# Where the matmul operands of a two-layer encoder start in SBUF, modulo 256 bytes

## The chip, the core and the metric

The kernel runs on one core of one Trainium2 chip. The metric is the device time of one execution in microseconds (us), lower is better. Engines are called PE (TensorE; its weight loads are a row of their own, PEld), DVE (VectorE), ACT (ScalarE), POOL (GpSimd) and SP (which here issues DMAs).

## The reference

A hybrid encoder trunk of two layers on two request groups of 256 tokens (512 tokens together, model width 1024), all in float32:

```python
def encoder_layer(x, c, cos, sin, p):
    ...
    h = rmsnorm(x, p['ln1_g']) * (1 + sc1) + sh1
    (q_down, kv_down, rg_x, rg_gate, gdn_qkv, gdn_z,
     gdn_alpha, gdn_beta, gates) = split_cols(h @ p['w_in'], IN_SPLITS)
    ...
    for n, o_n in enumerate((o_mla, o_rg, o_gdn)):
        term = gates[:, :, n] * (o_n @ p['w_branch'][n])
        mixed = term if mixed is None else mixed + term
    x = x + gt1 * (mixed @ p['w_out'])
    h2 = rmsnorm(x, p['ln2_g']) * (1 + sc2) + sh2
    up = dwconv_centred(h2 @ p['ffn_w_up'], p['ffn_conv_w'], p['ffn_conv_b'])
    u_lin, u_gate = jnp.split(up, 2, axis=-1)
    x = x + gt2 * ((jax.nn.silu(u_gate) * u_lin) @ p['ffn_w_down'])
    return x
```

The three branches are latent attention (MLA), a gated linear recurrence (RG-LRU) and a gated delta rule (GDN). Most of the arithmetic is products of a weight matrix with 512 columns of activations.

## The kernel before, in words

Activations lie transposed: 128 channels on the partitions, the 512 tokens along the row. Every weight matrix is cut into units of 128x128; all units of a layer stand in one list in the order in which they are used, eight units to a chunk. A chunk (128 x 1024 float32, 512 KB) is loaded by SP into one of three `raw` buffers (`prefetch`, L369), then split into two float32r parts (`split_chunk`, L375): ACT rounds it into `wh`, DVE subtracts and writes the rest into `wl`. Each of the two has two buffers that are used in turn. The split of a chunk is called when the unit that stands six units ahead of it is handed out (`AHEAD`). Activations are split in the same way: `hh`/`hl` (the normalised input), `ch`/`cl` and `oh`/`ol` (attention), `xch`/`xcl` and `goh`/`gol` (the other branches), `mh`/`ml` (the mixed branches) and `ah`/`al` (FFN).

`mm3` (L400) makes each unit's product out of three matmuls in one pass each: high weights with high activations, high weights with low activations, low weights with high activations. The weights are the stationary operand (loaded by LDWEIGHTS, 128 columns of 4 bytes), the activations are the moving operand (512 columns of 4 bytes; `gemm` takes 256 columns where a job works on one request group, `g` 0 or 1). Only the values of the attention (`values`, L780) turn this round: there the split weights move.

`SIZE` gives the units of a job, `JOBS` the order of jobs; `BRANCHES` has how often each job comes:

```python
SIZE = {"in6": 48, "gq": 8, "gk": 8, "gv": 8, "uq": 3, "uk": 2, "pad": 2, "uv": 8,
        "gate": 8, "br": 4, "x": 8, "g": 8, "b": 2, "z": 8, "out3": 24, "out": 8, "up3": 24, "up": 8,
        "down": NFF, "close": 0, "mid": 0, "close2": 0}
```

PE's instructions stand in a list written out by hand. Between the jobs' matmuls a small driver puts in the steps of the branches (attention, delta rule, norms, the modulation `mod`), each when a modelled clock has passed the waiting time that a table (`SLACK`) gives it. These steps run in float32 matmuls.

SBUF buffers come from pools that lie one behind the other in each partition; a buffer starts at a multiple of 32 bytes. The constants (`cs`, `pv` and others) end at byte 27,168, which is 32 modulo 256; the pools `xm`, `h` and `w` follow, and their buffers are multiples of 2,048 bytes. So `hh`, `hl`, `raw`, `wh` and `wl` all start at 32 modulo 256. The pool `small` behind them shifts what comes next. In the built program the split buffers that PE reads start at these places modulo 256:

| operand | role | before | after |
|---|---|---|---|
| `hh` `hl` `ch` `cl` `oh` `ol` `xch` `xcl` `goh` `gol` | moving | 32 | 0 |
| `mh` `ml` `ah` `al` | moving | 224 | 0 |
| `wh` first, second buffer | weights | 32, 32 | 128, 32 |
| `wl` first, second buffer | weights | 32, 32 | 192, 224 |

A unit's weights start at a multiple of 512 bytes within their buffer, and a request group's activations at 0 or 1,024, so the places of the table hold for each of them. The GDN's `kq`, both operands of `gdn_gram`, starts at 96 before and at 0 after.

Of the kernel before, what the change touches and what calls it, by code (L numbers as in the profile page):

```python
# [8 lines left out]
F32 = mybir.dt.float32  # L9
F32R = mybir.dt.float32r  # L10
# [8 lines left out]
P = 128  # L19
# [215 lines left out]
def _body(es, tc, nc, xT, cT, wall, wmod, pvec, fng, cst, rope, xinit, yT, dbg):  # L235
# [3 lines left out]
    depth = pvec.shape[1]  # L239

    cp = es.enter_context(tc.tile_pool(name="const", bufs=1))
    xp = es.enter_context(tc.tile_pool(name="xm", bufs=8))
    hp = es.enter_context(tc.tile_pool(name="h", bufs=1))
    wp = es.enter_context(tc.tile_pool(name="w", bufs=2))
    sp = es.enter_context(tc.tile_pool(name="small", bufs=1))
    mm = es.enter_context(tc.tile_pool(name="mm", bufs=3, space=PSUM))
    aux = es.enter_context(tc.tile_pool(name="aux", bufs=5, space=PSUM))
    dp = es.enter_context(tc.tile_pool(name="dr", bufs=2, space=DRAM))


    cs = cp.tile([P, NCC], F32, name="cs")
# [26 lines left out]
    def debug(name, ap):  # L278
        if dbg is None or name not in dbg:
            return  # L280
        o = nc.dram_tensor("dbg_" + name, tuple(ap.shape), F32, kind="ExternalOutput").ap()
        nc.sync.dma_start(o, ap)
# [78 lines left out]


    NRAW = 3
    state = {"l": 0, "u": 0, "piece": None, "job": ""}

    loads, pieces = {}, {}


    def prefetch(at):  # L369
        if at not in loads:  # L370
            loads[at] = wp.tile([P, UC * P], F32, name="raw", tag="raw", bufs=NRAW)
            nc.sync.dma_start(loads[at], wall[at])
        return loads[at]

    def split_chunk(at):  # L375
        if at not in pieces:
            raw = prefetch(at)
            loads.pop(at)
            wh = wp.tile([P, UC * P], F32R, name="wh", tag="wh", bufs=2)
            wl = wp.tile([P, UC * P], F32R, name="wl", tag="wl", bufs=2)  # L380
            A.copy(wh, raw)  # L381
            sub(wl, raw, f32(wh))
            pieces[at] = (wh, wl)
# [287 lines left out]
    for l in range(depth):  # L671
# [62 lines left out]
        def low_rank():  # L734
            yield SLACK["low_rank"]
            ps = aux_tile((P, 8), "ssq")
            for e in range(2):
                token_sums(ps[:, 4 * e:4 * e + 4], lr["sq"][e])
            x = mp.tile([P, 8], F32, name="lrx", tag="lrx")
            r = lr["r"] = mp.tile([P, 8], F32, name="lrr", tag="lrr")  # L740
            for e, n in enumerate((3, 2)):
                V.tensor_scalar(x[:, 4 * e:4 * e + 4], ps[:, 4 * e:4 * e + 4], 0.5 / (n * P), 0.5 * EPS, ALU.mult, ALU.add)
            rsqrt(r, x)
            yield SLACK["lr_diag"]
            rs = aux_tile(name="spread")
            spread(rs, r[:, 4:8])
            for i in range(2):
                t = lr["raws"][i]
                stt(t, t, pcol("kv_norm_g", i), rs, ALU.mult, ALU.mult)
                ch = mp.tile([P, T], F32R, name="ch", tag="c2", bufs=10)  # L750
                cl = mp.tile([P, T], F32R, name="cl", tag="c2", bufs=10)
                split(t, ch, cl, pool=True)
                ckv.append((ch, cl))
            ev_ckv.set(SLACK["low_rank_out"])
# [259 lines left out]
        for job in JOBS:  # L1014
# [40 lines left out]
            elif k == "close":  # L1055
                for t in range(8):
                    debug(f"K{t}_{l}", Kt[:, t, :])
                    debug(f"Q{t}_{l}", Qt[:, t, :])
                mstack.close()
                RT, RS = 8, 2  # L1060
                ap = stack.enter_context(tc.tile_pool(name="rg", bufs=1))
# [19 lines left out]
                gdn.gated(hd, zt, oh, ol)  # L1081
            elif k == "mid":
                drv.until(gdn.ev_o)
                g2stack.close()
                ostack = ExitStack()
                op_ = ostack.enter_context(tc.tile_pool(name="outp", bufs=1, side="right"))
# [14 lines left out]
            elif k == "out3":  # L1101
                for d, ps in enumerate(gemms(ms_, 3)):
                    out_row(ps, d, 2)
            elif k == "out":
                d, g = ix
                out_row(gemm(ms_, g), d, g)
                if (d, g) == (7, 0):
                    h2 = {}
                    drv.spawn(early(l, 1, x1, sq, range(E2), h2, op_))
                elif (d, g) == (7, 1):  # L1110
                    wait(SLACK["norm"])
                    for us in sq.scale(1):
                        wait(us)
                    for k in range(8):
                        for g in ((1,) if k < E2 else (0, 1)):
                            modulated(l, 1, x1[k], sq.r[g], k, g, h2, op_, 4)
                    wait(SLACK["normed"])
                    drv.drain_spare()
                    ostack.close()
                    rstack.close()  # L1120
                    fstack = ExitStack()
                    fp = fstack.enter_context(tc.tile_pool(name="ffn", bufs=1))
            elif k == "up3":
                for n, ps in enumerate(gemms(hs(h2), 3)):
                    up(ps, n)
                if not last:
                    drv.spawn(mod_gen(l + 1, ((0, 1),), SLACK["mod2"]))
            elif k == "up":
                up(gemm(hs(h2)), ix[0])
            elif k == "down":  # L1130
                d, g = ix
                if d == 0:
                    sq = Norm(fp, 3)
                    if not last:
                        setup(l + 1)
                        xdram = dp.tile([P, 8, T], F32, name="xdram", tag="xdram")

                        def hraw(i):
                            half = []
                            for e in range(2):  # L1140
                                tag = "h%s%d" % ("hl"[e], i % 8)
                                t = hp.tile([P, T], F32, name="hraw", tag=tag)
                                nc.sync.dma_start(t, wmod[l + 1, i][:, e * T:(e + 1) * T])
                                half.append(t)
                            return tuple(half)
                        preload(l + 1, (2, 3), hraw)
                ps = gemm(acts, g)
                t = x1[d]
                for e in ((0, 1) if g == 2 else (g,)):
                    c = GS[e]  # L1150
                    stt(t[:, c], ps[:, c], modA[:, 3, d, e:e + 1], t[:, c], ALU.mult, ALU.add)
                    if not last:
                        nc.scalar.dma_start(xdram[:, d, c], t[:, c])
                sq.put(t, d, g)
                if g:
                    debug(f"x2_{d}_{l}", t)
                if last and d < 7:
                    A.activation(t, t, AF.Copy, scale=fg[:, d:d + 1])
                if (d, g) == (7, 0):
                    h = {}  # L1160
                    drv.spawn(result(x1, sq, 0) if last else early(l + 1, 0, x1, sq, (), h, fp))
# [16 lines left out]
class GDN:  # L1178
# [15 lines left out]

    def gates(self, ab):
        V, A, G, PE = self.V, self.A, self.G, self.PE
        g1, C = self.g1, self.C
        yield SLACK["ab"]
        ps = self.aux_tile((P, 4, 80), "gates")
        for t in range(4):  # L1200
            PE.transpose(ps[:, t, :], ab[0:80, t * P:(t + 1) * P], self.ident[0:80, 0:80])
        al = g1.tile([P, 4, 8], F32, name="al_", tag="al_")
        self.g = g1.tile([P, 4, 8], F32, name="g_", tag="g_")
        self.beta = g1.tile([P, 4, 8], F32, name="beta", tag="beta")
        dtb = self.pcol("dt_bias").unsqueeze(1).to_broadcast([P, 4, 8])
        nea = self.pr["nea"].unsqueeze(1).to_broadcast([P, 4, 8])
        V.tensor_tensor(al, ps[:, :, 64:72], dtb, ALU.add)
# [8 lines left out]
        for k, (m, d) in enumerate((("incf", 0), ("incb", 1), ("strf", 0), ("strb", 1))):  # L1216
            PE.matmul(pc[:, k, :], C(m), self.g[:, :, 4 * d:4 * d + 4], start=True, stop=True)

        self.negegc = g1.tile([P, 4, 4], F32, name="negegc", tag="negegc")
        self.ktail = g1.tile([P, 4, 4], F32, name="ktail", tag="ktail")  # L1220
        self.b1 = g1.tile([P, 4, 4], F32, name="b1", tag="b1")
        self.b2 = g1.tile([P, 4, 4], F32, name="b2", tag="b2")
        ex = g1.tile([P, 4, 16], F32, name="ex", tag="ex")
        A.activation(ex, pc, AF.Exp)
        exv = ex.rearrange("p k (g j h) -> p k g j h", g=2, j=2)
        bv = self.beta.rearrange("p (g j) e -> p g j e", j=2)
# [10 lines left out]

    def part(self, what, h, ps):
        V, A, G, PE = self.V, self.A, self.G, self.PE
        g1 = self.g1  # L1240
        if what == "q":
            self.heads[h] = dict(kq=g1.tile([P, 2, T], F32, name="kq", tag="kq", bufs=2),
                                 vt=g1.tile([P, 4, P], F32, name="vt", tag="vt", bufs=2),
                                 kd=g1.tile([P, 4, P], F32, name="kd", tag="kd", bufs=2),
                                 nrm=g1.tile([P, 3, 4], F32, name="nrm", tag="nrm", bufs=2),
                                 bR=g1.tile([P, 4, 2], F32, name="bR", tag="bR", bufs=2),
                                 ev_d=self.drv.event())
        hd = self.heads[h]
        c = g1.tile([P, T], F32, name="gc", tag="gc", bufs=2)
# [422 lines left out]
```

## Time and profile before

| | us |
|---|---|
| median of 3 runs (2043.85 to 2046.93) | 2044.58 |
| the profiled execution | 2049.36 |
| its span, first to last instruction | 2047.6 |
| PE busy in the span | 1988.4 |

The profile page gives busy time by engine and the chain of work that ended last; the trace answers with instructions in order of time, or grouped. A matmul's own time in the trace (0.39 us) is longer than the distance to the next one, because matmuls are pipelined: a stream's rate is read from the distance of starts.

### The profile page before, as it was taken

The numbers are of one execution on the slowest core, as the hardware profiler recorded it, in microseconds if no ns is written. First come the engines' busy times: TensorE is split into PE (matmuls) and PEld (weight loads), VectorE is DVE, ScalarE is ACT, GpSimd is POOL, SyncE is SP. The second block draws the span as 40 slices with busy tenths as digits, with TensorE's granted clock in tenths as the row PEclk, the third lists the DMA queues.
The fourth block names the chain that finished last, engine by engine and source line by source line (L and its number), as shares of the span: only waits on it lengthen the run. The fifth ranks groups of instructions, "written<-read, shape, count | busy, mean of one in ns | idle before, by whom it ended". The sixth has DMA issues, their size and how long they took to land.

```text
span 2047.6 us, 28679 instructions
## 1 busy us (share of the span) xinstructions
PE 1988.4 (97%) x11179; PEld 1560.5 (76%) x11179; DVE 1249.2 (61%) x2354; ACT 808.1 (39%) x1259; POOL 253.9 (12%) x519
## 2 busy tenths in 40 slices
PE   9999989999999999999999999799999999999998
PEld 4777756767787778888878777577678878888887
DVE  4675767744466766662357757785544677666434
ACT  3454355422333434442244534553323344444322
POOL 1100252222200100000011003523130010000000
PEclk9999999999999999999999999899999999999999
DMA  8232433334335343344333224333432533333333
GB/s 298 83 93 62 112 91 100 108 109 118 87 118 191 110 137 103 94 142 149 110 114 105 60 73 114 94 113 83 128 110 83 205 105 102 93 96 100 93 95 111
DMA packets 114135, 229.94 MB, mean 112 GB/s; under 512 B 52304, under 2 KB 57552, under 8 KB 114000
## 3 DMA queue, kind: packets, MB, share of 16 engines
q1 hardware_dynamic: 107376, 219.98, 35.9%
q10 hardware_dynamic: 6624, 8.14, 1.2%
q8 instruction: 88, 1.44, 0.3%
q14 instruction: 47, 0.39, 0.1%
HBM read 221.00 MB, written 7.08 MB: 111 GB/s over the span
## 4 chain that ended last, share of the span: by engine, by line
PE 84%; DVE 5%; POOL 4%; DMA 2%; issue 2%; ACT 2%; SPq 0%; POOLq 0%; DVEq 0%; ACTq 0%
PE mm_up L220 24%; PE mm_down L220 12%; PE mm_gate L220 11%; PE mm_br L220 6%; PE mm_out L220 4%; PE mm_in L220 3%; PE mod L220 3%; PE mm_z L220 2%; PE mm_gk L220 2%; PE mm_gv L220 2%; POOL xt L286 2%; POOL X L292 2%; PE mm_gq L220 2%; PE att_s L220 1%; PE gdn_rec L220 1%
## 5 line engine op out<-in xcount | busy, mean ns | idle before, releaser
L292 DVE TENSOR_TENSOR wl<-raw,wh 128x1024 fp32r<-128x1024 f32 x304 | 374.8, 1233 | 312.5 <-ACT wh L381 302.5
L381 ACT CAST wh<-raw 128x1024 fp32r<-128x1024 f32 x304 | 318.6, 1048 | 539.7 <-PE mm_down L220 131.9
L220 PE MATMUL mm_up<-hh,wh 128*128 128x512 f32 x704 | 277.0, 393 | 3.4 <-POOL hh L302 3.4
L220 PE MATMUL mm_up<-hl,wh 128*128 128x512 f32 x704 | 275.6, 391 | 0.0
L220 PE MATMUL mm_up<-hh,wl 128*128 128x512 f32 x704 | 275.4, 391 | 0.0
L295 DVE SCALAR_TENSOR_TENSOR cv<-mm_up,pv,cv 128x510 f32<-128x510 f32 x176 | 131.2, 748 | 68.4 <-ACT cv L544 65.3
L220 PEld LDWEIGHTS mm_up<-hh,wh 128*128 128x128 f32 x704 | 133.1, 189 | 38.1 <-issue 5.9
L220 PE MATMUL mm_gate<-hh,wh 128*128 128x512 f32 x384 | 160.7, 418 | 0.0
L220 PEld LDWEIGHTS mm_up<-hl,wh 128*128 128x128 f32 x704 | 133.0, 189 | 27.6 <-DVE hl L292 0.3
L220 PEld LDWEIGHTS mm_up<-hh,wl 128*128 128x128 f32 x704 | 132.9, 189 | 27.4
L220 PE MATMUL mm_gate<-hh,wl 128*128 128x512 f32 x384 | 150.3, 391 | 0.0
L220 PE MATMUL mm_gate<-hl,wh 128*128 128x512 f32 x384 | 150.3, 391 | 0.0
L220 PE MATMUL mm_down<-ah,wl 128*128 128x512 f32 (+1 forms) x396 | 146.1, 369 | 0.7 <-DVE wl L292 0.7
L220 PE MATMUL mm_down<-ah,wh 128*128 128x512 f32 (+1 forms) x396 | 146.1, 369 | 0.0
L220 PE MATMUL mm_down<-al,wh 128*128 128x512 f32 (+1 forms) x396 | 146.0, 369 | 0.0
L302 POOL TENSOR_SCALAR hh<-hn 128x256 fp32r<-128x256 f32 x64 | 34.0, 545 | 695.2 <-ACT hn L561 691.1
L544 ACT ACTIVATE cv<-mm_up,pv 128x512 f32<-128x512 f32 x88 | 68.4, 779 | 93.4 <-PE mm_up L220 93.4
L220 PEld LDWEIGHTS mm_gate<-hh,wh 128*128 128x128 f32 x384 | 72.3, 188 | 25.5 <-issue 12.5
L220 PEld LDWEIGHTS mm_down<-ah,wl 128*128 128x128 f32 x396 | 74.2, 187 | 15.1 <-DVE wl L292 0.9
L220 PEld LDWEIGHTS mm_down<-al,wh 128*128 128x128 f32 x396 | 74.3, 188 | 14.3
L220 PEld LDWEIGHTS mm_down<-ah,wh 128*128 128x128 f32 x396 | 74.2, 187 | 14.2
L220 PEld LDWEIGHTS mm_gate<-hh,wl 128*128 128x128 f32 x384 | 72.1, 188 | 16.1 <-DVE wl L292 0.2
(389 smaller groups left out, 3873.9 us busy)
## 6 DMA issues: line engine op xcount, KB each, us to landing
raw<-in_wall_dram SPq DMA_DIRECT2D x304, 512.0 KB, 3.6
raw<-in_wmod_dram SPq DMA_DIRECT2D x56, 512.0 KB, 3.7
mraw<-in_wmod_dram SPq DMA_DIRECT2D x16, 512.0 KB, 10.7
oraw<-in_wmod_dram SPq DMA_DIRECT2D x16, 512.0 KB, 7.5
hraw<-in_wmod_dram SPq DMA_DIRECT2D x16, 256.0 KB, 5.5
x<-in_xT_dram SPq DMA_DIRECT2D x8, 256.0 KB, 5.9
xr<-in_xT_dram ACTq DMA_DIRECT2D x8, 256.0 KB, 3.4
xdram<-x ACTq DMA_DIRECT2D x16, 128.0 KB, 2.3
```

What stands on the lines that cost most here:

```text
L220: return self.pe.matmul(out, lhsT, rhs, **kw)
L286: (eng or V).tensor_tensor(out, a, b, ALU.mult)
L292: (eng or V).tensor_tensor(out, a, b, ALU.subtract)
L295: V.scalar_tensor_tensor(out, a, s, b, op0, op1)
L302: G.tensor_scalar(hi, x, 1.0, 0.0, ALU.mult, ALU.add)
L381: A.copy(wh, raw)
L544: A.activation(dst, ps, AF.Identity, bias=bias, scale=w[lo])
```

## The change

No instruction is added, removed or moved: on all five engines the built program has the same instructions with the same waits in the same order; only SBUF addresses differ. The pool `small` moves ahead of `xm` and takes up the small buffers of the branches; unused fill buffers bring every pool to a multiple of 256 bytes. The two buffers of `wh` and of `wl` get names of their own, with fills between them, so that the four stand at four places.

```diff
     cp = es.enter_context(tc.tile_pool(name="const", bufs=1))
+    sp = es.enter_context(tc.tile_pool(name="small", bufs=1))
     xp = es.enter_context(tc.tile_pool(name="xm", bufs=8))
     hp = es.enter_context(tc.tile_pool(name="h", bufs=1))
     wp = es.enter_context(tc.tile_pool(name="w", bufs=2))
-    sp = es.enter_context(tc.tile_pool(name="small", bufs=1))
...
+    def fill(pool, size):
+        return pool.tile([P, size // 4], F32, name="fill", tag="fill", bufs=1)
+    fill(sp, 160)
+
+    fills = iter(range(8))
+
+    def shift(size):
+        wp.tile([P, size // 4], F32, name="fill", tag=f"fill{next(fills)}", bufs=1)
...
             loads[at] = wp.tile([P, UC * P], F32, name="raw", tag="raw", bufs=NRAW)
+            if not placed:
+                placed.append(True)
+                shift(128)
             nc.sync.dma_start(loads[at], wall[at])
...
-            wh = wp.tile([P, UC * P], F32R, name="wh", tag="wh", bufs=2)
-            wl = wp.tile([P, UC * P], F32R, name="wl", tag="wl", bufs=2)
+            b = state["buf"] = 1 - state["buf"]
+            wh = wp.tile([P, UC * P], F32R, name="wh", tag=f"wh{b}", bufs=1)
+            if not state["placed"][b]:
+                shift((64, 192)[b])
+            wl = wp.tile([P, UC * P], F32R, name="wl", tag=f"wl{b}", bufs=1)
+            if not state["placed"][b]:
+                shift((96, 32)[b])
+                state["placed"][b] = True
             A.copy(wh, raw)
             sub(wl, raw, f32(wh))
...
-            x = mp.tile([P, 8], F32, name="lrx", tag="lrx")
-            r = lr["r"] = mp.tile([P, 8], F32, name="lrr", tag="lrr")
+            x = sp.tile([P, 8], F32, name="lrx", tag="lrx")
+            r = lr["r"] = sp.tile([P, 8], F32, name="lrr", tag="lrr")
...
+                fill(mp, 96)
                 mstack.close()
...
+                fill(gdn.g2, 160)
                 g2stack.close()
...
+                    fill(op_, 224)
                     ostack.close()
```

The other lines of the diff move the GDN's small buffers (`al_`, `g_`, `beta`, `negegc`, `ktail`, `b1`, `b2`, `ex`, `nrm`, `bR`) from the pool `g1` to `small` in the same way.

## Rows read from the trace of the kernel before

**Rows 1.** Page, span and busy time by engine (us, share, instructions).

```profile
span 2047.6 us, 28679 instructions
PE 1988.4 (97%) x11179; PEld 1560.5 (76%) x11179; DVE 1249.2 (61%) x2354; ACT 808.1 (39%) x1259; POOL 253.9 (12%) x519
```

**Rows 2.** Page, the chain that ended last, by engine and by line.

```profile
PE 84%; DVE 5%; POOL 4%; DMA 2%; issue 2%; ACT 2%; SPq 0%; POOLq 0%; DVEq 0%; ACTq 0%
PE mm_up L220 24%; PE mm_down L220 12%; PE mm_gate L220 11%; PE mm_br L220 6%; PE mm_out L220 4%; PE mm_in L220 3%; PE mod L220 3%; PE mm_z L220 2%; PE mm_gk L220 2%; PE mm_gv L220 2%; POOL xt L286 2%; POOL X L292 2%; PE mm_gq L220 2%; PE att_s L220 1%; PE gdn_rec L220 1%
```

**Rows 3.** Busy us by stretch: PE, PEld, DVE, ACT, POOL, clock, DMA share, GB/s.

```profile
190.00:580.00 390.00, 371.56 (x2647) 284.12 (x2645) 235.14 (x461) 149.33 (x239) 103.41 (x216) 0.97 0.36 102
...
672.00:912.00 240.00, 240.00 (x1054) 191.52 (x1053) 159.37 (x205) 104.98 (x134) 3.20 (x5) 1.00 0.37 110
```

**Rows 4.** PE in order of time, FFN up: start us, length us, instruction.

```profile
821.30 0.39 PE L220 MATMUL mm_up<-hh,wh 128*128 128x512 f32 x1
821.52 0.39 PE L220 MATMUL mm_up<-hl,wh 128*128 128x512 f32 x1
821.75 0.39 PE L220 MATMUL mm_up<-hh,wl 128*128 128x512 f32 x1
...
823.34 0.39 PE L220 MATMUL mm_up<-hh,wh 128*128 128x512 f32 x1
```

**Rows 5.** PE in order of time, FFN down.

```profile
948.29 0.40 PE L220 MATMUL mm_down<-al,wh 128*128 128x512 f32 x1
948.52 0.40 PE L220 MATMUL mm_down<-ah,wl 128*128 128x512 f32 x1
948.76 0.39 PE L220 MATMUL mm_down<-ah,wh 128*128 128x512 f32 x1
...
950.39 0.39 PE L220 MATMUL mm_down<-al,wh 128*128 128x512 f32 x1
```

**Rows 6.** The chain in order of time: start us, us, pieces merged.

```profile
195.87 21.76 PE mm_br L220 x96
```

**Rows 7.** PE in order of time, warm-up (bfloat16), 16 matmuls merged.

```profile
7.75 3.62 PE L358 MATMUL warm<-zb 128*128 128x512 bf16 x16
```

**Rows 8.** PE in order of time, float32 products of the GDN, merged.

```profile
266.69 0.81 PE L220 MATMUL gdn_gram<-kq 128*128 128x256 f32 x3
```

**Rows 9.** PE's weight loads in order of time, where mm_up gives way to mod.

```profile
746.72 0.19 PEld L220 LDWEIGHTS mm_up<-hl,wh 128*128 128x128 f32 x1
746.95 0.19 PEld L220 LDWEIGHTS mm_up<-hh,wl 128*128 128x128 f32 x1
747.49 0.14 PEld L220 LDWEIGHTS mod<-raw,csil 128*32 128x32 f32 x4 [0.35 <-issue]
```

**Rows 10.** The tile mm_up in 747.36 to 747.47 us: length ns min/median/max.

```profile
L220 PE MATMUL mm_up<-hh,wl x1: 389/389/389, 747.2 to 747.2; 128*128 128x512 f32 x1
```

**Rows 11.** PE in order of time, five matmuls after a step of the GDN.

```profile
441.11 0.40 PE L220 MATMUL mm_gk<-hl,wh 128*128 128x512 f32 x1
441.34 0.39 PE L220 MATMUL mm_gk<-hh,wl 128*128 128x512 f32 x1
441.57 0.40 PE L220 MATMUL mm_gk<-hh,wh 128*128 128x512 f32 x1
441.80 0.39 PE L220 MATMUL mm_gk<-hl,wh 128*128 128x512 f32 x1
442.03 0.39 PE L220 MATMUL mm_gk<-hh,wl 128*128 128x512 f32 x1
```

**Rows 12.** Page, costliest groups: the split, and two of PE's (busy, mean ns).

```profile
L292 DVE TENSOR_TENSOR wl<-raw,wh 128x1024 fp32r<-128x1024 f32 x304 | 374.8, 1233 | 312.5 <-ACT wh L381 302.5
L381 ACT CAST wh<-raw 128x1024 fp32r<-128x1024 f32 x304 | 318.6, 1048 | 539.7 <-PE mm_down L220 131.9
L220 PE MATMUL mm_up<-hl,wh 128*128 128x512 f32 x704 | 275.6, 391 | 0.0
```

**Rows 13.** Page, DMA issues: the weight chunks (KB each, us to landing).

```profile
raw<-in_wall_dram SPq DMA_DIRECT2D x304, 512.0 KB, 3.6
```

**Rows 14.** What PE itself waited for: us, times, longest us.

```profile
PE gdn_l L220 <- DVE W L289: 12.6, 2, 6.4
PE gdn_rec L220 <- DVE Y L1466: 10.9, 2, 5.4
```

More of the change, by code (lines that the diff above doesn't have):

```diff
@@ L363, in _body @@
     NRAW = 3
-    state = {"l": 0, "u": 0, "piece": None, "job": ""}
-    loads, pieces = {}, {}
+    state = {"l": 0, "u": 0, "piece": None, "job": "", "buf": 1, "placed": [False, False]}
+    loads, pieces, placed = {}, {}, []
     def prefetch(at):
@@ L1196, in gates @@
         V, A, G, PE = self.V, self.A, self.G, self.PE
-        g1, C = self.g1, self.C
+        sp, C = self.sp, self.C
         yield SLACK["ab"]
@@ L1201, in gates @@
             PE.transpose(ps[:, t, :], ab[0:80, t * P:(t + 1) * P], self.ident[0:80, 0:80])
-        al = g1.tile([P, 4, 8], F32, name="al_", tag="al_")
-        self.g = g1.tile([P, 4, 8], F32, name="g_", tag="g_")
-        self.beta = g1.tile([P, 4, 8], F32, name="beta", tag="beta")
+        al = sp.tile([P, 4, 8], F32, name="al_", tag="al_")
+        self.g = sp.tile([P, 4, 8], F32, name="g_", tag="g_")
+        self.beta = sp.tile([P, 4, 8], F32, name="beta", tag="beta")
         dtb = self.pcol("dt_bias").unsqueeze(1).to_broadcast([P, 4, 8])
@@ L1217, in gates @@
             PE.matmul(pc[:, k, :], C(m), self.g[:, :, 4 * d:4 * d + 4], start=True, stop=True)
[L1219 to L1223, printed above, removed]
+        self.negegc = sp.tile([P, 4, 4], F32, name="negegc", tag="negegc")
+        self.ktail = sp.tile([P, 4, 4], F32, name="ktail", tag="ktail")
+        self.b1 = sp.tile([P, 4, 4], F32, name="b1", tag="b1")
+        self.b2 = sp.tile([P, 4, 4], F32, name="b2", tag="b2")
+        ex = sp.tile([P, 4, 16], F32, name="ex", tag="ex")
         A.activation(ex, pc, AF.Exp)
@@ L1239, in part @@
         V, A, G, PE = self.V, self.A, self.G, self.PE
-        g1 = self.g1
+        g1, sp = self.g1, self.sp
         if what == "q":
@@ L1244, in part @@
                                  kd=g1.tile([P, 4, P], F32, name="kd", tag="kd", bufs=2),
-                                 nrm=g1.tile([P, 3, 4], F32, name="nrm", tag="nrm", bufs=2),
-                                 bR=g1.tile([P, 4, 2], F32, name="bR", tag="bR", bufs=2),
+                                 nrm=sp.tile([P, 3, 4], F32, name="nrm", tag="nrm", bufs=2),
+                                 bR=sp.tile([P, 4, 2], F32, name="bR", tag="bR", bufs=2),
                                  ev_d=self.drv.event())
```

## The prediction

> **What bounds the kernel now.** I read the page first. PE is busy for 1988.4 of 2047.6 us [rows 1], and the chain that ended last is PE for 84%; its largest lines are plain weight products, mm_up, mm_down, mm_gate, mm_br and mm_out [rows 2]. DVE and ACT have room: 61% and 39% [rows 1]. By stretches, the FFN up stage has PE busy for all of its 240 us at a granted clock of 1.00, the upper level of 2.4 GHz; the branch stage leaves PE idle for 18 of 390 us [rows 3]. So the time hangs on how fast one matmul follows another, and that is read from starts in order of time.
>
> In mm_up nine steps take 823.34 - 821.30 = 2.04 us, 226.7 ns each [rows 4]. In mm_down nine steps take 950.39 - 948.29 = 2.10 us, 233.3 ns each [rows 5]. The two streams have one form: 512 moving columns of 4 bytes, 128 columns of weights, the clock at its upper level. Weights begin at 32 modulo 256 in both; the moving operand begins at 32 in mm_up and at 224 in mm_down. mm_br, whose activations also begin at 32 but come from other buffers, has 21.76 / 96 = 226.7 ns [rows 6]. So the level goes with the place, not with the buffer or the job: a place costs 6.6 ns per matmul here.
>
> What is the best possible? Streams that read half as many bytes per ns run faster. The bfloat16 warm-up, 512 columns of 2 bytes, does fifteen steps in 3.62 - 0.38 us, 216 ns each [rows 7] (0.38 is one matmul's own length). The float32 products, 256 columns of 4 bytes, take (0.81 - 0.38) / 2 = 215 ns, although their operands lie at 96 modulo 256 [rows 8]. So 215.6 ns is a floor for 512 columns of work, and the float32r streams stand 11.1 and 17.7 ns above it. Whether a float32r stream can reach that floor at any place, no row shows.
>
> **The change, part by part.** It changes addresses alone, so its whole effect is in lengths.
>
> *Moving operands from 32 or 224 to 0.* How many matmuls? From the table of unit sizes, a layer has in6 48, twelve GDN projections 96, uq 18, uk 8, gate 192, br 96, x, g and z 32 each, b 16 and up 352 units: 922, and the attention's values with 24 matmuls count as 8. That is 930 x 3 x 2 layers = 5,580 matmuls at 32 (mm_up alone has 704 of each of its three forms, in agreement [rows 12]). At 224: down 154 and out 48 units with 512 columns, 202 x 3 x 2 = 1,212. The 456 matmuls of 256 columns would give half a step each, 1.5 us at most; I leave them out.
>
> The length at 0 is unknown, so bounds: below, the floor of 215.6 ns [rows 7, 8]; above, the worse of the two places seen, 233.3 ns [rows 5]. Zero lies 32 bytes from either place seen, so neither is nearer. Both places seen lie 32 past a multiple of 64; a stream that begins on a whole multiple of every power of two up to 256 cuts no unit of reading of such a size, and the two half-rate streams show that nothing else keeps 512 columns from 215.6. I therefore take a value on the lower side, but not the floor: one more step of the size seen between the two places, 226.7 - 6.6 = 220.1 ns. Saving: 5,580 x 6.6 = 36.8 us, and 1,212 x 13.2 = 16.0 us; together 52.8 us.
>
> *The weights' four buffers from 32 to 128, 192, 32 and 224.* Does a weight load slow the stream under it? Where mm_up gives way to mod, PE's next weight load starts only at 747.49 us, when the stream has passed, and the loads' row is empty for 0.35 us before [rows 9]. The matmul in that gap takes 389 ns [rows 10] against a mean of 391 with a load under it [rows 12]. So the loads cost 2 ns at most at this distance, and I put the new places at nothing, with 0 to 2 ns x 6,792 = 0 to 14 us of gain as the small bound. In the other direction I use the unsettled stream: just after a step of the GDN the same matmuls follow each other at (442.03 - 441.11) / 4 = 230 ns before they settle [rows 11]. Four different places could keep a stream from settling. That is the rival below.
>
> The Trainium skill, in "SBUF — State Buffer", section "Who interferes with whom", says that PE and ACT never wait on anyone; by it the place of an operand would not matter and the sum would be zero. The trace here differs: 226.7 against 233.3 ns for one form [rows 4, 5].
>
> *Small buffers to another pool, fills.* No instruction is added and the waits are the same. Cost nothing.
>
> *What hides the rest.* Faster matmuls need weights sooner. A chunk serves 24 matmuls, 5.28 us at 220 ns. Its split takes ACT 1.05 and DVE 1.23 us [rows 12], called 18 matmuls, 4.0 us, ahead; its load lands in 3.6 us with three buffers [rows 13]. Both stay covered; uncovered, each chunk would cost up to 2.3 us, 304 times. What is late next are the branch steps: 16% of the chain is not PE [rows 2], and PE already waits for DVE at the GDN's W and Y, up to 6.4 us at once [rows 14]. Where such a chain leads, faster filler matmuls only lengthen the wait. I keep 84% of the saving: 52.8 x 0.84 = 44.4 us.
>
> Sum: the profiled execution took 2049.4 us (span 2047.6, 1.8 around it), so 2005.0 us; it stands 4.8 us above the median of the runs shown, so 2000 us beside that median.
>
> **The rivals.**
>
> *Full rate.* At 0 the stream reaches the floor: 5,580 x 11.1 + 1,212 x 17.7 = 61.9 + 21.5 = 83.4 us, of which 84% is 70 us: 1974 us (1961 if none is given back). For it: two kinds of stream do run at 215.6 [rows 7, 8]. Against it: they read half the bytes. The Trainium skill, in "TensorE: Matmul & The Clock Gate", section "Back-to-back issue gap", gives columns / 2.4 + 2.5 ns, an estimate of 215.8 ns for 512 columns; by it this would be the case. The warm-up agrees [rows 7], mm_up does not [rows 4].
>
> *Only the worse streams gain.* 226.7 is what float32r can do, and 0 is as good as 32. Then 1,212 x 6.6 = 8.0 us, in stages that are PE alone: 2037 us. For it: mm_br and mm_up agree to 0.1 ns [rows 4, 6].
>
> *Nothing happens.* 2044.6 us. The two streams would have to differ by something other than place. Against it: nothing else differs in form or clock.
>
> *Slower.* The streams do not settle, because the distance between moving operand and weights now changes with every pass from wh to wl and every chunk, while before all four buffers stood at one place. At 230 to 231 ns throughout [rows 11] this costs 5,580 x 4.0 = 22 us and gives back 1,212 x 2.8 = 3 us: 2064 us. If instead 0 is as bad as 224, it is 5,580 x 6.6 = 37 us: 2081 us. The case decides from 227.9 ns on, the mean of before, (5,580 x 226.7 + 1,212 x 233.3) / 6,792. For it: a disturbed stream does run slower, and no row shows what a change of the weights' place does in a settled one. Against it: a matmul without a load under it is hardly shorter [rows 10], so loads seem not to set the rate.
>
> **How the numbers follow.** One step lower, 2000 us: 0.36 (its own range 1985 to 2020). Full rate, 1974: 0.28. Only the worse streams, 2037: 0.09. Nothing: 0.07. Slower, 2064 to 2081: 0.20. A measurement of this kernel tells about 0.2% (4 us) from no change. Faster by more than that: 0.36 + 0.28 + 0.09 = 0.73; within: 0.07; slower: 0.20. The range runs from 1961, the full rate with nothing given back, to 2070, which leaves out the worst slower case and half of its middle: 1961 to 2070 us.
>
> **What would show it.** Starts in mm_up and mm_down: one common distance, near 220 ns (215.6: full rate; 226.7: only the worse streams; alternating or over 228: slower). mm_br's piece of 96 in the chain near 21.1 us. The same count of instructions, the split's lengths unchanged. PE's waits at W and Y longer by some us each, the share of PE in the chain a little lower. Wrong would be: a distance that differs between the first and second wh buffer or between wh and wl, which would mean that the loads' place decides after all; or a shorter distance with a time that does not follow, since the branch steps took it.

## The result, and the profile after

The changed kernel takes 2063.67 us (median of 4 runs, 2061.25 to 2064.38) beside 2044.69 us before: ratio 1.0091, 95% interval 1.0079 to 1.0103. It is slower by 19 us, where I had forecast 2000 us. The time lies inside the stated range of 1961 to 2070 us, but on the other side of no change.

The page of the changed kernel: PE has 15 us more to do than in [rows 1], and the other engines have what they had. PE's share of the chain is 85% (84% in [rows 2]).

```profile
span 2059.5 us, 28679 instructions
PE 2003.6 (97%) x11179; PEld 1557.9 (76%) x11179; DVE 1250.1 (61%) x2354; ACT 808.4 (39%) x1259; POOL 256.2 (12%) x519
...
PE 85%; POOL 4%; DVE 4%; DMA 3%; issue 2%; ACT 2%; SPq 1%; POOLq 0%; DVEq 0%; ACTq 0%
...
L303 DVE TENSOR_TENSOR wl<-raw,wh 128x1024 fp32r<-128x1024 f32 x304 | 374.0, 1230 | 319.1 <-ACT wh L401 309.0
L401 ACT CAST wh<-raw 128x1024 fp32r<-128x1024 f32 x304 | 317.8, 1046 | 543.1 <-PE mm_down L220 131.4
```

The split's two instructions are as long as in [rows 12]. Now the chain in order of time (start us, us, what), first three pieces of the kernel before that were not shown yet, then the same of the changed kernel:

```profile
585.65 21.76 PE mm_br L220 x96
...
1670.36 241.07 PE mm_up L220 x1056
1911.43 118.35 PE mm_down L220 x555
```

```profile
194.59 22.29 PE mm_br L220 x96
...
582.67 22.30 PE mm_br L220 x96
...
1676.36 247.27 PE mm_up L220 x1056
1923.63 118.33 PE mm_down L220 x555
```

mm_br answers to [rows 6]: 22.29 / 96 = 232.2 ns between starts, not 226.7. The second layer's mm_up takes 6.2 us more. mm_down, which I had expected to gain most, stays within 0.02 us: from start to start its wide matmuls go from 233.3 to 232.2 ns, its narrow ones (256 columns) from 115.8 to 119.5. PE in order of time in mm_down of the changed kernel, beside [rows 5]:

```profile
1002.83 0.39 PE L220 MATMUL mm_down<-al,wh 128*128 128x512 f32 x1
1003.05 0.39 PE L220 MATMUL mm_down<-ah,wl 128*128 128x512 f32 x1
1003.28 0.40 PE L220 MATMUL mm_down<-ah,wh 128*128 128x512 f32 x1
1003.52 0.39 PE L220 MATMUL mm_down<-al,wh 128*128 128x512 f32 x1
...
1006.78 0.39 PE L220 MATMUL mm_down<-ah,wh 128*128 128x512 f32 x1
```

Seventeen steps take 3.95 us, 232.4 ns each, and they are not equal: read in ns from the trace they lie between 227 and 241. Both streams now have one common mean, as forecast for streams whose moving operands all begin at 0, but it is 232 ns and not 220.

In the branch stage little of the loss shows. From the first mm_br to the second of layer one it was 585.65 - 195.87 = 389.8 us before [rows 6] and is 582.67 - 194.59 = 388.1 us now; in layer two it was 388.0 us and is 389.0. The stretch of layer one by engines, before and after:

```profile
195.90:585.60 389.70, 371.26 (x2645) 283.88 (x2644) 236.91 (x463) 149.35 (x239) 103.41 (x216) 0.97 0.36 103
```

```profile
194.60:582.70 388.10, 370.53 (x2645) 281.48 (x2645) 237.41 (x463) 149.32 (x239) 104.77 (x216) 0.98 0.37 103
```

PE stands idle for 18.4 us before and for 17.6 us after, so longer matmuls took the place of waits for 0.8 us at most. The granted clock was lower before, 0.97 against 0.98, which can hide a loss of some us; how much of it arrives in this stage is open. In the FFN the loss shows plainly.

### The profile page after: what moved, and what is told of

Read it like the earlier page. It is cut to its first block, busy times and chain, and to the rows that moved or that the text cites. A ratio compares the mean times of both kernels' runs of the same rounds, so it can differ in the third digit from the quotient of the medians.

```text
span 2059.5 us, 28679 instructions
## 1 busy us (share of the span) xinstructions
PE 2003.6 (97%) x11179; PEld 1557.9 (76%) x11179; DVE 1250.1 (61%) x2354; ACT 808.4 (39%) x1259; POOL 256.2 (12%) x519
## 4 chain that ended last, share of the span: by engine, by line
PE 85%; POOL 4%; DVE 4%; DMA 3%; issue 2%; ACT 2%; SPq 1%; POOLq 0%; DVEq 0%; ACTq 0%
PE mm_up L220 24%; PE mm_down L220 12%; PE mm_gate L220 11%; PE mm_br L220 6%; PE mm_out L220 4%; PE mm_in L220 3%; PE mod L220 3%; PE mm_z L220 2%; PE mm_gk L220 2%; PE mm_gv L220 2%; POOL X L303 2%; POOL xt L297 2%; PE mm_gq L220 2%; DMA raw<-in_wall_dram 2%; PE att_s L220 1%
## 5 line engine op out<-in xcount | busy, mean ns | idle before, releaser
L220 PE MATMUL mm_up<-hh,wh 128*128 128x512 f32 x704 | 282.0, 401 | 3.4 <-POOL hh L313 3.4
```

The costliest lines, as they stand in the source:

```text
L220: return self.pe.matmul(out, lhsT, rhs, **kw)
```

## The experiments

The theory after the result: what counts is neither the moving operand's place nor the weights' place, but the **distance** from the one to the other modulo 256 (the weights' start minus the moving operand's). Before, it was 0 for 5,580 matmuls (226.7 ns once settled) and 32 - 224 = 64 for 1,212 (233.3 ns). Rivals: a moving operand at 0 has a length of its own; or any constant place settles well, and only the change from buffer to buffer costs.

**One place for all four weight buffers, moving operands at 0.** The edit of the changed kernel for w64 (the others have another first and last fill; w0 has none, which is the change's moving-operand part alone):

```diff
-                shift(128)
+                shift(64)
...
-                shift((64, 192)[b])
+                shift((0, 0)[b])
...
-                shift((96, 32)[b])
+                shift((0, 192)[b])
```

A fill of size 0 is left out.

> All moving operands at 0, all four weight buffers at 0 modulo 256, so the distance between them is 0, as in the 5,580 matmuls of the kernel before that ran at 226.7 ns. Distance theory: 226.7 ns between starts in mm_up and mm_down alike, time 2044.7 - 1,212 x 6.6 = 2037 us. Moving-place theory (a moving operand at 0 has a length of its own, whatever the weights): mm_up as in the changed kernel, 232 ns, time near 2064 us. Unsettled theory (any place does, only the change of places costs): 227 ns or less, 2037 us or less.

> Moving operands at 0, all four weight buffers at 64: the distance that the 1,212 matmuls with ah, al, mh, ml had before (32 - 224 = 64 modulo 256) at 233.3 ns. Distance theory: 233.3 ns everywhere, time 2044.7 + 5,580 x 6.6 = 2081 us. Moving-place theory: 232 ns, 2064 us. Unsettled theory: 227 ns or less, 2037 us.

> Moving operands at 0, all four weight buffers at 128. In the changed kernel a matmul with a load from 128 under it took 230 to 235 ns. Distance theory: one settled length, not 226.7 nor 233.3 by necessity; by those rows 230 to 237 ns, 2055 to 2095 us. Moving-place theory: 232 ns, 2064 us. Unsettled theory: 227 ns or less, 2037 us.

> Moving operands at 0, all four weight buffers at 192. In the changed kernel a matmul with a load from 192 under it took 231 ns, one with a load from 224 under it 230 ns. Distance theory: one settled length, by those rows 226 to 231 ns, 2034 to 2060 us. Moving-place theory: 232 ns, 2064 us. Unsettled theory: 227 ns or less, 2037 us.

> Moving operands at 0, all four weight buffers at 32. Distance theory, as the four runs so far bear it out (0: 226.7 ns, 64: 233.3, 128: 232.3, 192: 229.0): between its neighbours 0 and 64, 227 to 235 ns; the changed kernel had 234.4 ns with loads from 32 following each other, so 234 ns, near 2075 us. A rival, that only the part of the place above 64 counts: as w0, 226.7 ns, 2039 us.

> Moving operands at 0, all four weight buffers at 96. Distance theory: between its neighbours 64 (233.3) and 128 (232.3): 230 to 235 ns, 2055 to 2080 us. Rival, only the part above 64 counts: as w64, 2072 us with its two lengths of 231 and 236 ns in turn.

> Moving operands at 0, all four weight buffers at 160. Distance theory: between its neighbours 128 (232.3) and 192 (229.0): 229 to 233 ns, 2045 to 2066 us. Rival, only the part above 64 counts: as w128, a cycle of seven lengths, 2065 us.

> Moving operands at 0, all four weight buffers at 224. Distance theory: between its neighbours 192 (229.0) and 0 (226.7): 225 to 230 ns, 2033 to 2050 us; if any distance beats 0 it is this one. Rival, only the part above 64 counts: as w192, lengths of 226, 229 and 232 ns in turn, 2046 us.

Finer places are made by a buffer 64 elements longer, of which a slice is used:

```diff
-            wh = wp.tile([P, UC * P], F32R, name="wh", tag=f"wh{b}", bufs=1)
+            wh = wp.tile([P, UC * P + 64], F32R, name="wh", tag=f"wh{b}", bufs=1)[:, 4:4 + UC * P]
```

(w16; `wl` likewise; w240 begins at element 60, w8 at 2, w248 at 62.)

> Moving operands at 0, all four weight buffers at 16 (the distance 0 gave 226.7 ns, 32 gave 233.3). Theory that the place counts in 32-byte pieces: as w0, 226.7 ns, ratio 0.997. Theory that each 16 bytes count: another length, 227 to 235 ns, or one below 226.7; ratio 0.98 to 1.012.

> Moving operands at 0, all four weight buffers at 240, 16 bytes before a multiple of 256 (224 gave 233.3 ns, 0 gave 226.7). Theory of 32-byte pieces: as w224, 233.3 ns, ratio 1.012. Theory that each 16 bytes count: another length, 225 to 235 ns; ratio 0.99 to 1.015.

> Moving operands at 0, all four weight buffers at 8. 0 gave 226.7 ns and 16 gave 232.5. Theory that places count in 16-byte lines: as w0, 226.7 ns, ratio 0.997. Theory that they count byte by byte: between the two, 227 to 232 ns, ratio 0.997 to 1.007.

> Moving operands at 0, all four weight buffers at 248. 240 gave 228.1 ns with single steps of 225 and 226, 0 gave 226.7. Theory of 16-byte lines: as w240, 228.1 ns, ratio 0.996. Theory that they count byte by byte: between, or a place below 226, 225 to 228 ns, ratio 0.990 to 0.997.

Measured; the third column is the chain's first piece of 96 mm_br divided by 96:

| weights at | ratio to before (95%) | ns between starts in mm_br |
|---|---|---|
| 0 | 0.9968 (0.9957 to 0.9979) | 226.7 |
| 8 | 1.0054 (1.0039 to 1.0069) | 230.6 |
| 16 | 1.0079 (1.0053 to 1.0105) | 233.3 |
| 32 | 1.0104 (1.0087 to 1.0122) | 233.3 |
| 64 | 1.0132 (1.0116 to 1.0147) | 233.3 |
| 96 | 1.0130 (1.0115 to 1.0146) | 234.3 |
| 128 | 1.0104 (1.0087 to 1.0120) | 232.3 |
| 160 | 1.0116 (1.0100 to 1.0132) | 233.3 |
| 192 | 1.0007 (0.9996 to 1.0018) | 228.9 |
| 224 | 1.0118 (1.0101 to 1.0135) | 233.3 |
| 240 | 0.9959 (0.9945 to 0.9974) | 228.3 |
| 248 | 1.0126 (1.0111 to 1.0141) | 233.3 |

The chain in order of time of w0: mm_br at 226.7 ns as before, and the second layer's mm_down 2.5 us shorter than the 118.35 of before.

```profile
197.53 21.76 PE mm_br L220 x96
...
1662.89 241.10 PE mm_up L220 x1056
1904.00 115.87 PE mm_down L220 x555
```

The same of w64: mm_br at 22.40 / 96 = 233.3 ns, mm_up 7.2 us longer than before, and mm_down exactly as before, when it had the same distance at another place.

```profile
196.75 22.40 PE mm_br L220 x96
...
1686.80 248.30 PE mm_up L220 x1056
1935.10 118.35 PE mm_down L220 x555
```

The mean lengths agree with the distance theory in these two: 0 gives 226.7 ns whether the moving operand is at 0 or at 32, 64 gives 233.3 whether it is at 0 or at 224. The agreement at 64 is weak evidence by itself, since six of the twelve places give 233.3, and the single steps differ: 231 and 236 ns in turn in w64, 232 to 235 in the mm_down of before. The moving-place theory falls, since the moving operands are at 0 in all twelve. The unsettled theory falls too: eleven constant places cost 228.3 to 234.3 ns, eight of them at least as much as the four changing ones. The time of w64 rises by 26 us where 37 were expected; step 5 below says why.

A stream that the experiments were not made for tests the theory further. The attention's values (mm_uv) turn the operands round: the weights move, and the activations, at 0, are loaded. So with the weights at 64 their distance is 0 - 64 = 192, and with the weights at 192 it is 64. Twelve steps in w64, then in w192:

```profile
122.73 0.39 PE L220 MATMUL mm_uv<-wh,cl 128*128 128x512 f32 x1
...
125.48 0.39 PE L220 MATMUL mm_uv<-wh,cl 128*128 128x512 f32 x1
```

```profile
122.24 0.40 PE L220 MATMUL mm_uv<-wh,cl 128*128 128x512 f32 x1
...
125.04 0.40 PE L220 MATMUL mm_uv<-wh,cl 128*128 128x512 f32 x1
```

They take 2.75 / 12 = 229.2 ns in w64, whose other streams have 233.3, and 2.80 / 12 = 233.3 ns in w192, whose other streams have 228.9: the two lengths have changed places, as the distance says. The values of w96 (distance 160) have 233.3 ns and those of w160 (distance 96) 234.6, which also fits. For places finer than 32 bytes the distance alone is not enough: the values of w248 have distance 8 but 233.3 ns, not the 230.6 of w8, and those of w16 have distance 240 but 231.7 ns, not the 228.3 of w240.

```profile
122.78 0.39 PE L220 MATMUL mm_uv<-wh,cl 128*128 128x512 f32 x1
...
125.58 0.39 PE L220 MATMUL mm_uv<-wh,cl 128*128 128x512 f32 x1
```

(w248: 2.80 / 12 = 233.3 ns.)

My guesses for places not yet seen were mixed. w32, w96, w16, w240 and w8 fell into their ranges, but w224 and w160 came out slower than expected, and w248 is worse than both its neighbours at 240 and 0. So the rate is no smooth function of the place, and it counts bytes finer than 16: 8 differs from both 0 and 16. The rivals that only the part above 64 counts, or only whole pieces of 32 or of 16 bytes, fall with 32, with 16 and with 8.

The mean of the changed kernel's four places agrees with the table: of three matmuls, two load from wh and one from wl, so the first pair (128, 192) would give (2 x 232.3 + 228.9) / 3 = 231.2 ns, the second (32, 224) 233.3, and the mean is 232.2, which is what its mm_br shows. Chunk by chunk it does not come out. Chunks take the two pairs in turn, 24 matmuls each; by their count in the list of units, the first of these stretches of the second layer's mm_up has the first pair, the next one the second:

```profile
1786.91 0.40 PE L220 MATMUL mm_up<-hh,wh 128*128 128x512 f32 x1
...
1792.51 0.39 PE L220 MATMUL mm_up<-hh,wh 128*128 128x512 f32 x1
...
1798.06 0.40 PE L220 MATMUL mm_up<-hh,wh 128*128 128x512 f32 x1
```

The first pair has 5.60 / 24 = 233.3 ns and the second 5.55 / 24 = 231.3 ns, and so it is in chunk after chunk. So the rate under loads that change between two places is not the average of the two constant ones, and that the mean agrees is not shown to be more than luck.

**The other part alone.** The kernel before, with ah, al, mh and ml brought to 32, where its weights are:

```diff
+    sp.tile([P, 16], F32, name="fill", tag="fill", bufs=1)
     mm = es.enter_context(tc.tile_pool(name="mm", bufs=3, space=PSUM))
...
         g1 = stack.enter_context(tc.tile_pool(name="g1", bufs=1))
+        g1.tile([P, 48], F32, name="fill", tag="fill", bufs=1)
...
+                    op_.tile([P, 48], F32, name="fill", tag="fill", bufs=1)
                     ostack.close()
```

> The kernel before with one part of the change alone: fills bring mh, ml, ah and al from 224 to 32 modulo 256, the distance 0 that all other split matmuls have already; weights and all else stay. Distance theory: mm_down and the wide mm_out go from 233.3 to 226.7 ns, 1,212 x 6.6 = 8.0 us, time 0.4% below the kernel before (ratio 0.996). Rival, that mm_down is slower for another reason than its place (its buffers, its job): 233.3 ns stays, ratio 1.000.

Measured: ratio 0.9965 (0.9954 to 0.9977), 2039.99 us. Its chain in order of time has the mm_down of w0:

```profile
193.73 21.76 PE mm_br L220 x96
...
1906.51 115.87 PE mm_down L220 x555
```

So mm_down was slow for its places, not for its job. The gain is 7.2 us (4.7 to 9.4). Of the 8.0 us expected, something is paid back by the 456 narrow matmuls, which I had left out: they are shorter at distance 64. Grouped by form, of the kernel before and of w0 (a matmul's own mean length in ns second last):

```profile
L220 PE MATMUL mm_down<-al,wh 128*128 128x256 f32 x88 | 24.5, 278 | 0.0
```

```profile
L220 PE MATMUL mm_down<-al,wh 128*128 128x256 f32 x88 | 24.9, 283 | 0.0
```

From start to start the trace has 115.6 ns before and 120.8 in w0 and in ffn32, so 5.2 ns x 456 = 2.4 us. w0, ffn32 and w240 beat both kernels; their intervals overlap, so which of the three is best is not settled.

**Is it the load?** In bcast each load of the kernel before reads one column 128 times, so the products are of other numbers; instructions and moving operands stay.

```diff
-        return wh[:, o:o + P], wl[:, o:o + P]
+        return wh[:, o:o + 1].to_broadcast([P, P]), wl[:, o:o + 1].to_broadcast([P, P])
```

> The kernel before, but each weight load reads one column of the unit 128 times instead of its 128 columns, so the products are of other numbers: the load no longer sweeps through addresses, while instructions, counts and moving operands stay. Theory that the sweeping load holds up the stream at any distance, least at 0: the stream reaches the floor of 215.6 ns that the half-rate streams show, 62 + 21 us less, 1961 to 1975 us. Rival, that 226.7 ns is what a float32r stream takes by itself: 226.7 ns in mm_up and mm_down, 2037 us. Third, that the loads do not matter at all (as I had argued from the matmul without a load under it): 226.7 and 233.3 ns as before, 2045 us.

Measured: ratio 1.0054 (1.0038 to 1.0070). All three expectations missed. The chain of before, first layer, then that of bcast:

```profile
914.62 110.79 PE mm_down L220 x489
```

```profile
196.23 22.19 PE mm_br L220 x96
...
916.42 109.78 PE mm_down L220 x489
```

mm_br has gone up to 22.19 / 96 = 231.1 ns. mm_down has gone down: 109.78 us where the same 489 took 110.79 before. From start to start, mm_up has 230.7 ns and the wide mm_down 231.4, where before they had 226.8 and 233.3. So the addresses that the loads read make most of the difference between the two streams, which shrinks from 6.5 to 0.7 ns when each load stays at one place; but a load without a sweep is no better than a load at a poor distance.

In half, which is ffn32 except that all matmuls of a group after its first use only 64 of the 128 columns (half of the output channels lack their later terms), each load is half as long:

```diff
+        if first:
+            PE.matmul(ps, w[0], x[0], start=True, stop=False, skip_group_check=True)
+        else:
+            PE.matmul(ps[0:64], w[0][:, 0:64], x[0], start=False, stop=False, skip_group_check=True)
+        PE.matmul(ps[0:64], w[0][:, 0:64], x[1], start=False, stop=False, skip_group_check=True)
+        PE.matmul(ps[0:64], w[1][:, 0:64], x[0], start=False, stop=last, skip_group_check=True)
```

> The kernel with all split operands at distance 0 (ffn32), but in each group all matmuls but the first load and multiply only the first 64 of the unit's 128 columns, so half of the output channels lack their later terms; the moving streams are the same 512 columns, each load is half as long. Theory that the loads hold the 11 ns above the floor too: about half of it goes, 221 ns between starts with a 64-column load under the stream, 5,580 + 1,212 matmuls x 5.5 = 37 us less than ffn32, ratio near 0.98. Rival, that 226.7 ns is the float32r stream's own rate: 226.7 ns, ratio 0.996 as ffn32.

Measured: ratio 1.0011 (1.0002 to 1.0021), against 0.9965 for ffn32. Weight loads in order of time, beside the 0.19 us of [rows 9], and a piece of the chain:

```profile
822.23 0.13 PEld L220 LDWEIGHTS mm_up<-hh,wh 128*64 128x64 f32 x1
822.46 0.13 PEld L220 LDWEIGHTS mm_up<-hl,wh 128*64 128x64 f32 x1
```

```profile
195.05 22.08 PE mm_br L220 x96
```

The loads are shorter, and the stream is slower: 22.08 / 96 = 230.0 ns. Both expectations missed. So the 11 ns between 226.7 and the floor do not shrink with the length of the load, and a shorter load at distance 0 even loses the good rhythm. The edit also halves the output rows of these matmuls, so it does not change the load alone. The narrow matmuls go the other way: 114.3 ns from start to start against 120.8 in ffn32.

## Why the prediction was wrong, step by step

1. *PE's rate bounds the kernel; place moves it by 6.6 ns; the sum goes by matmuls times ns.* Right in the counts and in the two levels, which come back in w0 and w64. But 226.7 is the level of a settled stream; in the branch stage, where steps of the branches break in, the same matmuls had 228.6 ns before.
2. *Moving operands from 32 or 224 to 0: one step lower, 220.1 ns, 52.8 us.* Wrong, and this is the first step that failed. No run shows 220.1 ns as the mean of such a stream. [Rows 4] and [rows 5] differ in the moving operand's place, but with the weights at 32 in both they differ in the distance as well; I read the first and did not think of the second. That the half-rate streams reach 215.6 ns does not show that only the place keeps a float32r stream from it, since they also read half the bytes. With the distance kept at 0, the move to 0 alone gives 226.7 ns in mm_up, mm_down and mm_br alike (w0), which was my third case: 2037 us forecast, 2039 measured.
3. *The weights' four places cost nothing.* Wrong, and this decides the sign. I had taken the length of one matmul without a load under it, 389 ns [rows 10], as a sign that loads do not matter. That row gives a matmul's own length, not the distance to the next start, and one matmul in a settled stream says nothing about a stream under other loads. From distance 0 to the four new ones mm_br goes from 226.7 to 232.2 ns; w0, which differs from the changed kernel in these places alone, takes 2039 us and not 2064. The prediction had named the sign for this, a distance that differs between the first and the second wh buffer, and the chunks of the changed kernel show it.
4. *The rival "slower", 2064 us.* Its time came true, and its price per matmul (230 to 231 ns) was near, but its mechanism did not: constant places are as slow as changing ones. The places cost, and their change showed no cost of its own in the mean. That the time agrees to 1 us is luck: its 19 us are 2.8 ns for each of the 6,792 matmuls, where the mean rose by 3.3, and all of it was taken to arrive.
5. *84% of a change in PE's work reaches the end.* About right, beside a sum that was too large. From 226.7 to 232.2 ns in 5,580 matmuls, less 1.1 ns in 1,212, would be 29 us, of which 19 is two thirds. But the branch stage's matmuls started from 228.6, not 226.7. Over all steps between neighbouring wide matmuls at a granted clock of 1.00 the mean went from 228.8 to 232.1 ns: 3.3 x 6,792 = 22 us, of which 19 is 85%. In w64 the same mean is 233.3, which is 30 us, and 26 arrived.
6. *The split and the loads stay covered; no instruction is added.* Right.

What stays open: why distance 0 is among the best of those tried, why 240 and 192 are near it and 248 is not, what counts beside the distance below 32 bytes, and what holds a wide float32r stream at 226.7 ns when half-rate streams reach 215.6 [rows 7, 8]. Shorter loads did not free it (half); a run without any load was not tried, since every matmul here carries one.

## What to carry to other kernels

Read a matmul stream's rate from the distance of starts, stage by stage, and where two stages of one form differ, compare both operands' start addresses before blaming either one. When a change moves two things whose difference may count, run each alone first: w0 beside the changed kernel shows that the alignment gains 0.3% and the staggering takes 1.2%. If float32r matmuls with 512 columns bound a kernel, put weights and moving operands at the same place modulo 256 bytes, and measure; three fills do it here.

## What the runs showed of the hardware that was not expected

- With 512 moving float32r columns and a 128-column load under them, at a granted clock of 1.00, the places of the two operands' starts modulo 256 bytes set 226.7 to 234.3 ns between starts. For places that are multiples of 32 the mean went with the distance between the two, in the streams and in the values that turn them round; for finer places the distance alone did not settle it (w248, w16). The Trainium skill, in "TensorE: Matmul & The Clock Gate", section "Step-by-step: what each phase is for", says that loading the next tile's weights doesn't steal SBUF read bandwidth from the running matmul. These runs show that the load is not without effect: between w0 and w64 only the weights' place differs, and the lengths between starts differ by 6.6 ns. Whether read bandwidth is the reason, no run here shows.
- The streams fall into fixed cycles. The starts in the trace of w64 are 231 and 236 ns apart in turn, those of w192 226, 229 and 232, those of w128 repeat after seven; w0 holds one length. No step between two wide matmuls at a granted clock of 1.00 was below 223 ns in any run.
- Narrow streams order the distances differently: the 256-column matmuls start 120.8 ns apart at distance 0, and 115.6 (before) and 117.3 (w64) at distance 64.
